# The pad at the top of SBUF of a decoder trunk grows from 96 to 224 bytes

## The chip, the cores and the metric

The kernel runs on one core of a Trainium2 chip. The metric is the device time of one execution in microseconds (us); the time of a kernel is the median of its runs. A profile comes from one further execution, whose own time is given beside it. In the profile PE is TensorE (matmuls), PEld its weight loads, DVE is VectorE, ACT is ScalarE, POOL is GpSimd, SP is SyncE, which issues most DMAs.

## What is computed

A decoder trunk of one layer on 1024 tokens of width 1024, in float32: an RMS norm, two token mixers in parallel (a gated linear recurrence and a chunked linear attention) merged by gates, an output projection and a residual; then a norm, a squared-ReLU MLP with 4096 hidden channels, a residual and a last norm. Cut to its frame:

```python
def reference(x, ..., norm_mix, ..., norm_mlp, w_up, w_down, norm_final):
    h = rms_norm(x, norm_mix)
    x = x + hybrid_mixer(h, ...)                       # w_in: 1024 x 8192, then w_out
    h = rms_norm(x, norm_mlp)
    x = x + jnp.square(jax.nn.relu(h @ w_up)) @ w_down # 1024 x 4096, 4096 x 1024
    return rms_norm(x, norm_final)
```

## The kernel before

**Three matmuls for one product.** TensorE multiplies in a shortened float32 (fp32r). Every operand is therefore split in two (`split`, L75 to L77): H is the value cast to fp32r on ACT (L76), L is what the cast lost, made on DVE (L77). `mm3` (L113) then makes each product from three matmuls into the same PSUM bank: H·H (L115), stationary times moving as they are named, then the two mixed terms (L116, L117). Nearly all matmuls have a stationary operand of 128x128 (512 bytes of a partition's row) and a moving operand of 128x512 (2048 bytes). Before each matmul TensorE loads the stationary operand of the next one, while the matmul in flight reads its moving operand, both from SBUF.

**Stages.** The mixer takes the tokens in two halves of 512 (`hT0`, `hT1`), each in four pairs of heads: projections `pj_*` with weights `w` stationary and the normed input `hT` moving, the gates of the recurrence (`pr`, `pi`, with `xcH` and `xcL` moving), then scans and small matmuls. The output projection (`po`) follows, and the second norm (`second_norm`, L686), which leaves the MLP's input in SBUF.

The MLP multiplies by quads of 2x2 blocks with seven products in place of eight. The table `PLAN` (L658) names for each of the seven steps the PSUM bank (X, Y, Z), the combination of weights (A11, s1, s2, s3, s4, A12, A22) and that of the input (B11, t1, n2, B21, T3, B22, T4). A combination of weights is made from four raw blocks by DVE sums and then split (`quad_steps`, L749).

- *Up* (`hidden`, L804): 16 quads one after the other. For each quad seven steps, each of four slices by three matmuls, 84 in all. The weights are stationary, the input h2 (14 tiles, `h2B11H` to `h2T4L`) moves. While quad q runs, DVE and ACT prepare the weights of quad q + 1, empty the banks of q (`e`, `b`) and split the hidden values of q − 1 (`hidden_ops`), which go to DRAM for all quads but the last two.
- *Down* (L936): eight blocks of two quads, 168 matmuls each. Now the hidden values `u` are stationary and the weights move. Of each two quads, one lives in the pools on the left of SBUF, the other in those on the right (`side`, L901); for each product and each block of rows, six matmuls (two row blocks by three) of the left quad are followed by six of the right one. In the last half of the last block a row block stands alone, and the sides change after three. DVE adds each bank to the accumulators (`acc`, L963). `u` and weights of the next two quads come by DMA meanwhile.

**Who lies where.** The pools on the left of SBUF grow upward from low addresses, those opened with `side="right"` grow down from the top of the 224 KiB of a partition. The mixer's tiles are all on the left. Ahead of the MLP's pools on the right a tile named `pad` is taken (L673, L674) that nothing reads or writes; it pushes down everything opened on the right after it. Tiles of 2048, 4096 and 8192 bytes follow one another there, so all of them share one residue mod 512. The addresses of the built program:

| tiles | side | byte of the first | residue mod 512 before | after |
|---|---|---|---|---|
| weights `w` of the mixer, of up and of the left down quads | left | 23296 to 47872 | 256 | 256 |
| `hT`, `y` (moving or stationary in the mixer), `xcH` at 170752, `xcL` at 174848 | left | 47872 to 174848 | 256 | 256 |
| the input of up, `h2*` | right | 114560 (before) | 384 | 256 |
| `u` of the left down quads | left | 56064 to 80640 | 256 | 256 |
| `u`, weights and raw blocks of the right down quads, `acc` | right | 98176 (before) and up | 384 | 256 |

Order on each engine: program order with hints of priority; PE runs its queue in order, and DMAs of weights and of `u` go out on SP's queue.

Of the kernel before, what the change touches and what calls it, by code (L numbers as in the profile page):

```python
# [10 lines left out]
F32 = mybir.dt.float32  # L11
# [7 lines left out]
P = 128  # L19
# [22 lines left out]
def trunk(ctx: ExitStack, tc: tile.TileContext, x, wts, mlp, pv, gains, mask_f, mask_u, out):  # L42
# [8 lines left out]
    def opened(name, **how):  # L51
        cm = tc.tile_pool(name=name, bufs=1, reuse_waits="tile", **how)
        return cm.__enter__(), lambda: cm.__exit__(None, None, None)
# [617 lines left out]


    pad, close_pad = opened("pad", side="right")  # L673
    pad.tile([P, 24], F32, tag="pad", name="pad")  # L674

    h2p = [opened(f"h2{i}", side="right") for i in range(4)]
    HOME = {"T4": 0, "B22": 0, "T3": 0, "B21": 1, "n2": 2, "t1": 2, "B11": 3}
# [371 lines left out]
```

## Time and profile before

| what | value |
|---|---|
| median of three runs | 1626.46 us (1626.07 to 1626.98) |
| the profiled execution, time around all | 1627.6 us |
| its span, first to last instruction | 1625.8 us |
| mean granted TensorE clock | 0.996 |
| mixer, output projection and second norm | to 987 us |
| up | 987 to 1309 us, 1344 matmuls |
| down | 1304 to 1618 us, 1344 matmuls |

How to read what follows: a group of instructions is given by its line, engine, operation, tiles written and read (out<-in), shape and count, then its total busy time and the mean ns of one. The ends of matmuls are modelled, so a matmul of 389 ns starts its successor earlier than that; the pace is the distance between starts. The view of stretches gives, for each piece of the span, its length, then for PE, PEld, DVE, ACT and POOL the busy time with the count of instructions that touch the piece, then the granted clock (1.00 is full), the share of DMA and GB/s. Waits are given as who waited for whom, in us in total, times, and the longest one. L numbers are lines of the kernel printed above.

### The profile page before, as it was taken

What the parts mean: (1) busy time and instruction counts of PE and PEld (TensorE: products, weight loads), DVE (VectorE), ACT (ScalarE), POOL (GpSimd) and SP (SyncE); (2) the same over time, 40 slices, a digit from 0 to 9 for tenths busy, and PEclk for the clock granted to TensorE, in tenths of its full rate; (3) what the DMA queues carried; (4) which work ended last, traced back from release to release, by engine and by line L of the source; (5) the groups of instructions that cost most, each with busy time, mean ns of one, the idle gap of its engine ahead of it and who ended that gap; (6) DMA issues with size and microseconds to landing.
All of it is one profiled execution on the core that took longest, in us unless ns stands there. A gap on an engine that the chain in (4) does not pass through costs nothing.

```text
span 1625.8 us, 23177 instructions
## 1 busy us (share of the span) xinstructions
PE 1583.0 (97%) x9240; PEld 1306.5 (80%) x9240; DVE 1212.2 (75%) x1751; ACT 764.6 (47%) x1186; POOL 65.0 (4%) x99
## 2 busy tenths in 40 slices
PE   7999999999999999999999997999999999999998
PEld 6788788788788788788787876888888877888886
DVE  5975956848764865848759688977777888788876
ACT  4643545435442544436434566766776732222113
POOL 0010100100100000000100100000000000000000
PEclk9999999999999999999999998999999999999999
DMA  6212212122243222222122362666656575666652
GB/s 237 91 66 91 92 66 104 66 91 92 79 167 135 86 78 90 80 78 103 67 91 91 117 207 104 248 248 250 237 233 246 223 269 213 256 255 247 256 209 104
DMA packets 57996, 246.51 MB, mean 152 GB/s; under 512 B 6688, under 2 KB 6816, under 8 KB 47136
## 3 DMA queue, kind: packets, MB, share of 16 engines
q1 hardware_dynamic: 56304, 239.27, 39.4%
q10 hardware_dynamic: 1584, 5.77, 1.0%
q8 instruction: 72, 1.18, 0.3%
q14 instruction: 36, 0.29, 0.1%
HBM read 185.24 MB, written 59.77 MB: 151 GB/s over the span
## 4 chain that ended last, share of the span: by engine, by line
PE 80%; DVE 15%; DMA 2%; issue 1%; ACT 1%; POOL 0%; DVEq 0%; POOLq 0%; SPq 0%; ACTq 0%
PE uX L115 3%; PE uX L117 3%; PE dX L115 3%; PE uX L116 3%; PE dX L117 3%; PE dX L116 3%; DVE wL L77 2%; PE pj_ga L117 2%; PE pv L116 2%; PE pv L117 2%; PE pv L115 2%; PE pj_ga L115 2%; PE pj_ga L116 2%; PE pj_f L117 2%; PE pj_ma L115 2%; PE pj_ma L117 2%
## 5 line engine op out<-in xcount | busy, mean ns | idle before, releaser
L77 DVE TENSOR_TENSOR wL<-raw,wH 128x1024 fp32r<-128x1024 f32 x160 | 194.3, 1214 | 150.0 <-ACT wH L76 145.8
L76 ACT CAST wH<-raw 128x1024 fp32r<-128x1024 f32 x160 | 167.8, 1049 | 166.3 <-issue 66.4
L963 DVE TENSOR_TENSOR acc<-acc,dX 128x512 f32<-128x512 f32 x128 | 85.1, 682 | 30.4 <-PE dX L117 29.7
L76 ACT CAST wA<-q 128x512 fp32r<-128x512 f32 x32 | 19.8, 621 | 129.0 <-PE dX L117 102.1
L963 DVE TENSOR_TENSOR acc<-acc,dY 128x512 f32<-128x512 f32 x64 | 43.5, 685 | 16.0 <-PE dY L117 15.1
L345 DVE RECIPROCAL rr<-rr 128x512 f32<-128x512 f32 x16 | 53.5, 3346 | 0.0
L823 ACT ACTIVATE b<-b 128x512 f32<-128x512 f32 x48 | 30.2, 631 | 38.4 <-DVE b L822 38.3
L115 PE MATMUL pv<-wH,hT0H 128*128 128x256 f32 x128 | 37.7, 294 | 0.0
L116 PE MATMUL pv<-wL,hT0H 128*128 128x256 f32 x128 | 37.4, 293 | 0.0
L117 PE MATMUL pv<-wH,hT0L 128*128 128x256 f32 x128 | 37.4, 292 | 0.0
L115 PE MATMUL pv<-wH,hT1H 128*128 128x256 f32 x128 | 36.5, 285 | 0.0
L116 PE MATMUL pv<-wL,hT1H 128*128 128x256 f32 x128 | 36.2, 283 | 0.0
L117 PE MATMUL pv<-wH,hT1L 128*128 128x256 f32 x128 | 36.2, 283 | 0.0
L311 DVE SCALAR_TENSOR_TENSOR xc<-xp,pvt,xc 128x512 f32<-128x512 f32 x48 | 33.1, 746 | 0.0
L551 ACT ACTIVATE on<-po 128x128 f32<-128x128 f32 x64 | 17.0, 278 | 33.4 <-PE po L541 33.2
L570 ACT ACTIVATE smb<-pj_mb 128x512 f32<-128x512 f32 x16 | 9.6, 597 | 45.4 <-PE pj_mb L117 45.2
L824 ACT ACTIVATE b<-b 128x512 f32<-128x512 f32 x48 | 30.0, 630 | 1.1
L77 DVE TENSOR_TENSOR wA<-q,wA 128x512 fp32r<-128x512 f32 x32 | 21.9, 686 | 10.5 <-ACT wA L76 10.3
L565 ACT ACTIVATE g<-pj_g 128x512 f32<-128x512 f32 x16 | 9.6, 599 | 37.3 <-PE pj_g L117 37.3
L444 POOL TENSOR_SCALAR seg<-seg 128x128 f32<-128x128 f32 (+1 forms) x16 | 12.7, 792 | 360.4 <-DVE seg L384 360.4
L384 DVE TENSOR_TENSOR seg<-seg 128x128 f32<-128x128 f32 (+2 forms) x96 | 26.7, 305 | 0.2
L117 PE MATMUL pj_ga<-hT1H,wL 128*128 128x512 f32 x64 | 26.5, 414 | 0.0
(1854 smaller groups left out, 5264.3 us busy)
## 6 DMA issues: line engine op xcount, KB each, us to landing
raw<-wts_in SPq DMA_DIRECT2D x160, 512.0 KB, 3.4
q<-mlp_in SPq DMA_DIRECT2D x64, 512.0 KB, 4.0
x<-x_in SPq DMA_DIRECT2D x8, 512.0 KB, 5.8
acc<-x ACTq DMA_DIRECT2D x8, 512.0 KB, 6.5
y_out<-acc SPq DMA_DIRECT2D x16, 256.0 KB, 2.1
xs<-x_in SPq DMA_DIRECT2D x8, 256.0 KB, 3.3
x<-xs SPq DMA_DIRECT2D x8, 256.0 KB, 2.4
x2s<-x_in SPq DMA_DIRECT2D x4, 512.0 KB, 4.4
```

Of the source, the lines that this page charges most:

```text
L76: keep(A.copy(h, src))
L77: keep(V.tensor_tensor(out=lo, in0=src, in1=h.bitcast(F32), op=ALU.subtract))
L115: PE.matmul(o, ah, bh, start=first, stop=False, **how)
L116: PE.matmul(o, ah, bl, start=False, stop=False, **how)
L117: PE.matmul(o, al, bh, start=False, stop=last, **how)
L311: V.scalar_tensor_tensor(xc[:, s, :], xp[:, j : j + T], pvt[:, PV_CW + 8 * j + u : PV_CW + 8 * j + u + 1], xc[:, s, :], op0=ALU.mult, op1= ...
L345: V.reciprocal(rec, rec)
L384: mul = lambda o, a, b: V.tensor_tensor(out=o, in0=a, in1=b, op=ALU.mult)
L551: A.activation(on[:, 4 * s + n, :], po[:, n * P : (n + 1) * P], AF.Square, accum_out=ssq[:, 4 * s + n : 4 * s + n + 1])
L823: A.activation(b[:, at, :], b[:, at, :], AF.Relu, scale=-1.0 if at == 2 else 1.0)
L824: A.activation(b[:, at, :], b[:, at, :], AF.Square)
L963: V.tensor_tensor(out=dst, in0=dst, in1=banks[bk, pr], op=op)
```

## The change

```diff
     pad, close_pad = opened("pad", side="right")
-    pad.tile([P, 24], F32, tag="pad", name="pad")
+    pad.tile([P, 56], F32, tag="pad", name="pad")
```

The pad has 56 float32 a partition in place of 24, which is 224 bytes in place of 96. Each of the 142 tiles on the right starts 128 bytes lower; each tile on the left stays. The two built programs have the same instructions in the same order on every engine, with the same waits; only the addresses differ.

## The prediction

> **What bounds the kernel now.** I read the page first, for who is busy and who ends the run.
>
> ```profile
> span 1625.8 us, 23177 instructions
> PE 1583.0 (97%) x9240; PEld 1306.5 (80%) x9240; DVE 1212.2 (75%) x1751; ACT 764.6 (47%) x1186; POOL 65.0 (4%) x99
> PE 80%; DVE 15%; DMA 2%; issue 1%; ACT 1%; POOL 0%; DVEq 0%; POOLq 0%; SPq 0%; ACTq 0%
> ```
>
> TensorE holds 80% of the chain that ended last. A busy PE is not a PE at its peak, so the question is at what pace matmuls of one shape (128x128 stationary, 128x512 moving) start. The change moves addresses and nothing else, so I compare stretches whose two operands lie differently. Next comes the view of stretches (length, then busy time and count of each engine, granted clock, DMA share, GB/s); the first stretch is mixer, two are the up half of the MLP, two the down half.
>
> ```profile
> 854.73:878.76 24.03, 24.03 (x107) 19.90 (x106) 21.71 (x26) 16.61 (x21) 0.00 (x0) 1.00 0.26 94
> 1201.17:1239.97 38.80, 38.80 (x169) 31.31 (x167) 30.68 (x39) 27.16 (x38) 0.00 (x0) 1.00 0.62 243
> 1240.27:1279.24 38.97, 38.97 (x168) 31.22 (x167) 30.75 (x39) 27.11 (x38) 0.00 (x0) 1.00 0.62 242
> 1354.38:1602.55 248.17, 248.17 (x1089) 204.64 (x1087) 197.85 (x289) 51.87 (x67) 0.00 (x0) 1.00 0.56 220
> 1590.00:1600.00 10.00, 10.00 (x45) 8.26 (x44) 6.22 (x13) 7.22 (x19) 0.00 (x0) 1.00 0.01 2
> ```
>
> PE never idles in them and the clock is full (1.00). The counts include one or two matmuls that straddle an edge, so the pace comes from the starts, here from the timeline of PE (start, duration, line, operation); I counted the starts between first and last row of each stretch: 106, 167, 167 and 1087.
>
> ```profile
> 854.73 0.39 PE L116 MATMUL pr<-xcL,wH 128*128 128x512 f32 x1
> 878.76 0.39 PE L116 MATMUL pj_g<-hT1L,wH 128*128 128x512 f32 x1
> ...
> 1201.17 0.39 PE L116 MATMUL uX<-h2T3L,ws310H 128*128 128x512 f32 x1
> 1239.96 0.47 PE L115 MATMUL uX<-h2T3H,ws312H 128*128 128x512 f32 x1
> 1240.27 0.40 PE L116 MATMUL uX<-h2T3L,ws312H 128*128 128x512 f32 x1
> 1279.24 0.44 PE L115 MATMUL uX<-h2T3H,ws314H 128*128 128x512 f32 x1
> ...
> 1354.38 0.40 PE L116 MATMUL dX<-ws116L,u0n 128*128 128x512 f32 x1
> 1602.55 0.43 PE L115 MATMUL dX<-ws128H,u12n 128*128 128x512 f32 x1
> ```
>
> Mixer: 24.03/106 = 226.7 ns from start to start. Up: 38.79/167 = 232.3 and 38.97/167 = 233.4 ns, mean 232.8. Down: 248.17/1087 = 228.3 ns. The addresses of the built program, in the table of placement above, sort these: in the mixer weights and moving operand both start at residue 256 mod 512, in up weights at 256 and h2 at 384, in down both at 256 for the quads kept on the left and both at 384 for those on the right, with a switch of side after every six matmuls. The switch can be seen in the groups by line of 1395 to 1436 us (mean ns of one last; L115, L116, L117 are the three matmuls of one product, u3 right side):
>
> ```profile
> L115 PE MATMUL dX<-ws119H,u3n 128*128 128x512 f32 x4 | 1.6, 391 | 0.0
> L116 PE MATMUL dX<-ws119L,u3n 128*128 128x512 f32 x4 | 1.6, 389 | 0.0
> L117 PE MATMUL dZ<-wA1219H,u3B 128*128 128x512 f32 x4 | 1.6, 392 | 0.0
> L115 PE MATMUL pi<-xcH,wH 128*128 128x512 f32 x32 | 12.4, 389 | 0.0
> L117 PE MATMUL uX<-h2B11H,wA 128*128 128x512 f32 x52 | 20.5, 395 | 0.0
> ```
>
> The durations are modelled, but they follow the pace: 389 where residues agree (mixer, and the middle matmul in down although both operands are at 384), 391 and 392 for the first and last ones, which meet a neighbour from the other side, 395 in up over 1040 to 1300 us. So it is the difference between the two residues that goes with the slower pace, not the residue 384 itself. Nor is it the high half of SBUF: the pi row reads xcH at byte 170752, weights below byte 48000, and has 389.
>
> **The change part by part.** The pad takes 128 bytes more, so everything in the pools on the right moves down by exactly 128 bytes: h2, the late u, the late weights, the late raw tiles and the accumulators go from residue 384 to 256. Order, waits and instructions of all engines stay the same. No operation is added or removed; the only price is the pace of matmuls.
>
> *Up, 1010 to 1284 us.* 1167 matmuls run there without a wait. At the mixer's pace each saves 232.8 − 226.7 = 6.1 ns: −7.1 us. Below I use −6.4 as the small end (0.6 ns each is kept) and −7.1 as the large one.
>
> *Down, 1354 to 1602 us.* No switch of residue is left: 1087 × (228.3 − 226.7) = −1.7 us; small end −1.4.
>
> *Restarts.* After a pause a matmul run takes a while to reach its pace even where residues agree. Two rows of a restart in the mixer, ten matmuls apart:
>
> ```profile
> 86.55 0.40 PE L115 MATMUL pj_mb<-hT0H,wH 128*128 128x512 f32 x1
> 88.86 0.39 PE L116 MATMUL pj_mb<-hT0L,wH 128*128 128x512 f32 x1
> ```
>
> 2.31 us for ten, 4.3 ns each over the settled pace, so some 0.04 us a restart. The two up stretches above are divided by such a pause (1239.96 to 1240.27); with five of them in up: +0.2 us, at most +0.5.
>
> *A loop that does not get faster.* That pause is PE waiting for the X bank, which ACT empties late (timeline of ACT, before the pause that begins at 1279.24):
>
> ```profile
> 1275.71 1.05 ACT L76 CAST ws115H<-s 128x1024 fp32r<-128x1024 f32 x1 [0.82 <-PE uX L116]
> 1276.67 1.04 ACT L76 CAST u13t<-b 128x1024 fp32r<-128x1024 f32 x1
> 1278.56 0.58 ACT L819 COPY e<-uX 128x512 f32<-128x512 f32 x1
> ```
>
> PE frees a buffer at 1275.71, ACT then works 3.43 us without pause to 1279.14, and PE does about 14 matmuls meanwhile. Those 14 shrink by 14 × 6.1 = 85 ns and ACT's 3.43 us do not, so each such wait may grow by 0.09 us. Seven pairs of quads: +0.6 us; between 0 (the wait is elsewhere) and +1.2 (every quad).
>
> *Stretches where PE's gain is lost.* Three waits end on other engines (waits, by total; and two stretches):
>
> ```profile
> PE uX L115 <- ACT ws30H L76: 1.7, 1, 1.7
> PEld dZ L116 <- DVE wA1230L L77: 1.6, 1, 1.6
> ACT wA L76 <- DMA q<-mlp_in: 17.8, 1, 17.8
> 1284.40:1312.90 28.50, 27.39 (x116) 21.25 (x114) 27.76 (x36) 21.47 (x31) 0.00 (x0) 1.00 0.61 221
> 1312.90:1354.10 41.20, 40.53 (x173) 32.11 (x173) 34.97 (x50) 10.38 (x13) 0.00 (x0) 1.00 0.75 287
> ```
>
> The first holds PE until 1009.6 whatever it did before (about 58 matmuls, 0.3 us). In 1284 to 1313 DVE is busy 27.76 of 28.50 us and PE waits for its last split, so 110 faster matmuls (0.6 us) only wait longer. In 1313 to 1354 the reloaded weights come 17.8 us late by DMA and PE pauses at the end (165 matmuls, 0.6 us). I take 0 for all three; if none were bound they would give 1.5 us.
>
> *Tail, 1602.8 to 1615.9 us.* Single row blocks, so the side switches every three matmuls:
>
> ```profile
> 1602.82:1615.85 13.03, 13.03 (x58) 10.48 (x56) 11.56 (x22) 4.10 (x12) 0.00 (x0) 1.00 0.36 135
> ```
>
> 13.03/56 = 232.7; aligned it saves 56 × 6.0 = 0.3 us, and DVE (11.56 of 13.03) takes some of it back: −0.15.
>
> Elsewhere the cover holds: DVE's 30.75 us and ACT's 27.11 us of a pair of quads must fit in 168 × 226.7 ns = 38.1 us instead of 39.3.
>
> Sum: −7.1 − 1.7 − 0.15 + 0.2 + 0.6 = −8.2 us. The profiled execution took 1627.6 us around its span of 1625.8, 1.1 above the median, and I carry the difference over: span 1617.6, median 1626.46 − 8.2 = **1618.2 us**. Large end: 7.1 + 1.7 + 0.3 + 1.5 = 10.6, 1615.8. Small end: 6.4 + 1.4 − 0.5 − 1.2 = 6.1, 1620.4.
>
> **The rivals.**
>
> *No change: addresses do not matter.* Up could be slower for another reason that mixer lacks: DMA at 0.62 against 0.26, or DVE and ACT writing. For it: nothing in the trace shows an address. Against it: down has DMA 0.56 over the long stretch and 0.01 in 1590 to 1600, and x45 in 10.00 us there is the same 228 pace; and in down 389 and 392 alternate with the side. Then 1626.5. The Trainium skill speaks for this rival. Its page "SBUF — State Buffer", section "Who interferes with whom", says that PE and ACT never wait on anyone, and "TensorE: Matmul & The Clock Gate", section "Step-by-step: what each phase is for", says that loading the next tile's weights does not steal SBUF read bandwidth from the running matmul; by them the residues could not matter and the sum would be 0. The 232.8 against 226.7 ns of equal shapes at full clock disagrees.
>
> *Only the switches go.* Up is slow for its own reason and keeps 232.8; down gains 1.7 and the tail 0.15: 1624.6. Against it: up and mixer have the same slices of 512 and 2048 bytes.
>
> *Slower: equal residues without settling.* The restart rows show that equal residues alone do not give 226.7; the two read streams first have to fall into step. If h2 at its new place never does, all 2254 matmuls of up and down run at one unsettled pace p. The change loses from p = 230.6 on (where 1167 × (232.8 − p) = 1087 × (p − 228.3)); at the 233.4 of the slower up stretch it costs 1167 × 0.6 + 1087 × 5.1 = +6.2 us: 1632.7. For it: the ten slow matmuls above. Against it: the mixer settles every time, in down both sides settle within a matmul or two of a switch.
>
> **How the numbers follow.** The main case gets 0.84, no change 0.06, only the switches 0.04, slower 0.06. The range is the main case's, 1615.8 to 1620.4; it leaves out the other cases (0.16) and little more. A measurement of this kernel tells about 0.2% (3.3 us) from no change; the main case lies beyond that even at its small end, the second and third within: faster 0.84, same 0.10, slower 0.06.
>
> **What would show it.** The up matmuls' mean falls from 395 to 389 ns and two quads take 38.1 to 38.4 us; in down L115, L116 and L117 all have 389. The waits at 1009.6 and for wA1230L grow by 0.3 to 0.6 us, that at the X bank by about 0.1 each. Mixer stretches and all DVE and ACT durations stay. It is wrong if up keeps 395 (another cause than residues), if the 389 comes but the span falls by under 6 us (another engine takes it), or if anything ahead of 977 us moves.

## The result and the profile after

| kernel | median, us | runs (lowest to highest) | ratio to before, 95% interval | span of the profiled run |
|---|---|---|---|---|
| before | 1626.35 | 6 (1625.81 to 1627.95) | | 1625.8 |
| after | 1619.67 | 6 (1618.12 to 1621.45) | 0.9958 [0.9946, 0.9971] | 1619.5 |

The changed kernel is faster, by 6.7 us in this first measurement. Two later ones gave 1626.91 to 1619.22 and 1627.33 to 1618.76 (both among the experiments), so 7.7 and 8.6 us; the mean of the three is 7.7. The forecast was 1618.2 us, 8.2 less than before.

The page of after, its span, its busy times and the chain that ended last:

```profile
span 1619.5 us, 23177 instructions
PE 1573.0 (97%) x9240; PEld 1302.9 (80%) x9240; DVE 1211.3 (75%) x1751; ACT 763.0 (47%) x1186; POOL 66.8 (4%) x99
PE 77%; DVE 17%; DMA 2%; ACT 2%; issue 2%; POOL 0%; DVEq 0%; POOLq 0%; SPq 0%; ACTq 0%
```

The instruction counts are those of before. PE is busy 10 us less; DVE, ACT and POOL are within 2 us of what they had. The stretches of after that answer to those of the prediction come next: mixer, two quads of up (the 167 starts from the same instruction to the same instruction), down (1087 starts), tail (56 starts).

```profile
855.28:879.33 24.05, 24.05 (x108) 19.90 (x106) 21.73 (x26) 16.62 (x21) 0.00 (x0) 1.00 0.28 93
1238.58:1276.55 37.97, 37.97 (x169) 31.16 (x167) 30.62 (x39) 26.93 (x38) 0.00 (x0) 1.00 0.64 247
1350.03:1596.48 246.45, 246.45 (x1089) 203.84 (x1087) 197.24 (x289) 51.84 (x67) 0.00 (x0) 1.00 0.56 221
1596.81:1609.61 12.80, 12.80 (x58) 10.44 (x56) 11.53 (x22) 4.10 (x12) 0.00 (x0) 1.00 0.35 136
```

The mixer is as before (24.05 against 24.03 us). Two quads of up went from 38.97 to 37.97 us, which is 233.4 to 227.4 ns a matmul; down from 248.17 to 246.45 us, 228.3 to 226.7 ns; the tail from 13.03 to 12.80 us. The groups by line say the same. First up (1040 to 1270 us) of after, then down (1390 to 1431 us) of after; the last number ahead of the second bar is the mean ns of one:

```profile
L115 PE MATMUL uX<-h2B11H,wA 128*128 128x512 f32 x48 | 18.7, 389 | 0.0
L117 PE MATMUL uX<-h2B11H,wA 128*128 128x512 f32 x48 | 18.7, 389 | 0.0
```

```profile
L115 PE MATMUL dX<-ws119H,u3n 128*128 128x512 f32 x4 | 1.6, 389 | 0.0
L117 PE MATMUL dZ<-wA1219H,u3B 128*128 128x512 f32 x4 | 1.6, 389 | 0.0
```

395 is gone from these rows of up, and 391 and 392 from those of down: they now have the mixer's 389. In up only the first matmuls behind a wait for the X bank stay longer (394 to 422 ns in the mean of four).

**Where the gain sits.** Five instructions cut the MLP into pieces. Their starts are in the timeline of PE (start, duration, line, operation; in brackets the wait ahead of it and who ended it). Before (the start of ws314H, 1279.24, stands in the prediction):

```profile
1009.62 0.51 PE L115 MATMUL uX<-h2T3H,ws30H 128*128 128x512 f32 x1 [1.72 <-ACT ws30H L76]
1312.91 0.50 PE L116 MATMUL dZ<-wA1230L,u14B 128*128 128x512 f32 x1 [1.12 <-DVE wA1230L L77]
1354.04 0.50 PE L115 MATMUL dX<-ws116H,u0n 128*128 128x512 f32 x1 [0.20 <-DVE acc L963]
1617.93 0.39 PE L117 MATMUL dX<-wA1229H,u13t 128*128 128x512 f32 x1
```

After, the profile of the first measurement:

```profile
1010.60 0.50 PE L115 MATMUL uX<-h2T3H,ws30H 128*128 128x512 f32 x1 [1.95 <-ACT ws30H L76]
1276.55 0.50 PE L115 MATMUL uX<-h2T3H,ws314H 128*128 128x512 f32 x1
1309.68 0.51 PE L116 MATMUL dZ<-wA1230L,u14B 128*128 128x512 f32 x1 [0.89 <-DVE wA1230L L77]
1349.69 0.50 PE L115 MATMUL dX<-ws116H,u0n 128*128 128x512 f32 x1 [0.28 <-DVE acc L963]
1611.73 0.40 PE L117 MATMUL dX<-wA1229H,u13t 128*128 128x512 f32 x1
```

After once more, the profile of its third measurement (e10):

```profile
1009.98 0.50 PE L115 MATMUL uX<-h2T3H,ws30H 128*128 128x512 f32 x1 [1.95 <-ACT ws30H L76]
1273.67 0.50 PE L115 MATMUL uX<-h2T3H,ws314H 128*128 128x512 f32 x1
1306.82 0.50 PE L116 MATMUL dZ<-wA1230L,u14B 128*128 128x512 f32 x1 [0.90 <-DVE wA1230L L77]
1347.03 0.50 PE L115 MATMUL dX<-ws116H,u0n 128*128 128x512 f32 x1 [0.25 <-DVE acc L963]
1609.13 0.39 PE L117 MATMUL dX<-wA1229H,u13t 128*128 128x512 f32 x1
```

Differences of these starts:

| piece | before | after | e10 | e10 − before |
|---|---|---|---|---|
| start to ws30H (mixer, norm, first product) | 1009.62 | 1010.60 | 1009.98 | +0.36 |
| ws30H to ws314H (up) | 269.62 | 265.95 | 263.69 | −5.93 |
| of it: starts up to 260 ns apart, excess over 226.7 | 6.95 | 0.31 | 0.22 | −6.73 |
| of it: starts further apart (waits), excess | 0.83 | 3.80 | 1.62 | +0.79 |
| ws314H to wA1230L | 33.67 | 33.13 | 33.15 | −0.52 |
| wA1230L to ws116H | 41.13 | 40.01 | 40.21 | −0.92 |
| ws116H to the last matmul (down) | 263.89 | 262.04 | 262.10 | −1.79 |

The third and fourth rows are sums over the 1155 distances between successive starts of that piece. The pace of up and of down is very nearly the mixer's in both profiles of after. What differs between these two profiles of one program, 2.3 us in up, lies in the starts that are further apart: in the first there is a stretch at half clock, and one raw block that came late. The view of stretches shows the first of these, two times 3 us from the start of ws30H, in after and then in e10 (the granted clock is the third number from the end):

```profile
1010.60:1013.60 3.00, 2.94 (x8) 2.12 (x9) 2.49 (x3) 0.00 (x0) 0.00 (x0) 0.69 0.04 5
1013.60:1016.60 3.00, 3.00 (x11) 2.35 (x11) 0.61 (x1) 0.00 (x0) 0.00 (x0) 0.74 0.91 341
```

```profile
1009.98:1012.98 3.00, 2.93 (x12) 2.10 (x13) 2.50 (x3) 0.00 (x0) 0.00 (x0) 1.00 0.02 1
1012.98:1015.98 3.00, 3.00 (x15) 2.48 (x14) 0.69 (x1) 1.36 (x3) 0.00 (x0) 1.00 0.93 345
```

The clock stays at 0.5 for some 3.4 us there (0.31 × 3 + 0.26 × 3 = 1.71 us of full clock are missing, which half clock takes 3.4 us to lose). Six matmuls start 0.42 to 0.43 in place of 0.23 us apart, the one ahead of them and the one behind are late too: the first 30 distances from ws30H on take 8.85 us, in e10 7.31, so the stretch takes 1.5 us.

### The profile page after: what moved, and what is told of

Read it like the earlier page. It is cut to its first block, busy times and chain, and to the rows that moved or that the text cites. A ratio compares the mean times of both kernels' runs of the same rounds, so it can differ in the third digit from the quotient of the medians.

```text
span 1619.5 us, 23177 instructions
## 1 busy us (share of the span) xinstructions
PE 1573.0 (97%) x9240; PEld 1302.9 (80%) x9240; DVE 1211.3 (75%) x1751; ACT 763.0 (47%) x1186; POOL 66.8 (4%) x99
## 4 chain that ended last, share of the span: by engine, by line
PE 77%; DVE 17%; DMA 2%; ACT 2%; issue 2%; POOL 0%; DVEq 0%; POOLq 0%; SPq 0%; ACTq 0%
PE dX L115 3%; PE dX L116 3%; PE dX L117 3%; PE uX L115 3%; PE uX L117 3%; PE uX L116 3%; DVE wL L77 2%; PE pj_ga L117 2%; PE pj_ga L116 2%; PE pj_ga L115 2%; PE pv L115 2%; PE pv L117 2%; PE pv L116 2%; PE pj_f L117 2%; PE pj_ma L117 2%; PE pj_ma L116 2%
```

## The experiments

Each kernel is compared with before in the same series. Residues are those of the built programs, mod 512 unless another is named.

**Again, unchanged (e1, e10).**

> The changed kernel once more, to see what of its profile is its own and what changes from run to run. If the wait on a weight load near 1199 us (1.1 us) and the half clock near 1012 us (3.4 us long) are chance, one or both are elsewhere or gone here and the median is 1618 to 1620 us; if the change itself brings them, both stand at the same place again and the span is within 1 us of 1619.5. Mixer stretches as before; up at 389 ns mean, 226.7 ns start to start.

> The kernel after, unchanged. Both theories: 1619.2 +- 0.7. If the half-clock stretch at 1009 to 1015 us comes with this program and not by chance, its profile shows it a third time, with the first matmul of ws31H some 1.2 to 1.5 us later against ws30H than in the run with both sides at 384.

Measured: e1 1619.22 us (1618.47 to 1620.25, 4 runs) against 1626.91, ratio 0.9950 [0.9935, 0.9965]; e10 1618.76 us (1617.81 to 1619.54, 5 runs) against 1627.33, ratio 0.9946 [0.9933, 0.9960]. The half-clock stretch is in the profile of e1, at 1009 to 1013 us, and not in that of e10. So it comes and goes with one program, and a single profile of after can be 1.5 us longer for it.

**Both sides at 384 (e2).** The old pad, and a tile that nothing uses at the bottom of SBUF, so that everything on the left rises by 128 bytes.

```diff
+    lpad = const.tile([P, 32], F32, tag="lpad", name="lpad")
...
-    pad.tile([P, 56], F32, tag="pad", name="pad")
+    pad.tile([P, 24], F32, tag="pad", name="pad")
```

> The pad stays at 96 bytes and everything on the left moves up by 128 bytes, so that both sides lie at residue 384. Theory (the difference of the residues of stationary and moving operand sets the pace): up at 226.7 ns start to start, 389 ns mean, in down L115, L116 and L117 all at 389, mixer unchanged, 1618 to 1621 us. Rival (384 is a bad residue, 256 a good one): up stays at 395 and the mixer rises from 389 to 395 too, over 1630 us.

Measured: 1618.01 us (1617.47 to 1619.20, 4 runs), ratio 0.9943 [0.9928, 0.9958]. Its two quads of up and its 1087 starts of down:

```profile
1235.16:1273.12 37.96, 37.96 (x168) 31.16 (x166) 30.62 (x39) 26.89 (x38) 0.00 (x0) 1.00 0.65 249
1346.71:1593.12 246.41, 246.41 (x1089) 203.84 (x1087) 197.17 (x289) 51.86 (x67) 0.00 (x0) 1.00 0.57 222
```

Both are those of after (37.97 and 246.45). All MLP operands on the right lie exactly where they lay before, at the residue 384; what moved is what they are multiplied with. So the place of an operand does not count, the distance between the two operands does.

**One half alone (e3, e4).** A second pad, opened just ahead of the late `u` (and so after h2), moves the tiles of the right down quads alone: in e3 back to residue 384 while h2 stays at 256, in e4 (with the old first pad) to 256 while h2 stays at 384.

```diff
+    pad2, close_pad2 = opened("pad2", side="right")
+    pad2.tile([P, 96], F32, tag="pad2", name="pad2")
...
-close_late_u, close_pad, close_ust
+close_late_u, close_pad2, close_pad, close_ust
```

That is e3; e4 has `[P, 32]` there and `[P, 24]` in the first pad.

> h2 at residue 256 as in the changed kernel, but a second pad of 384 bytes ahead of the late pools puts the right side of down back to 384. Theory: up at 389, down keeps 391, 389 and 392 (228.3 ns start to start), 1.5 to 2 us more than the changed kernel: 1620 to 1622.5 us. Rival (the gain of down comes from elsewhere, by its DMA or DVE): the same as the changed kernel, 1618 to 1620.

> h2 stays at residue 384, a second pad of 128 bytes ahead of the late pools puts the right side of down to 256. Theory: up keeps 395 (232.8 ns start to start), down L115, L116, L117 all 389 (226.7 ns), 1.5 to 2.5 us less than before: 1624 to 1625 us. Rival: down unchanged, 1626 to 1627.

Measured: up alone 1621.06 us (1620.29 to 1623.11, 5 runs), ratio 0.9964 [0.9950, 0.9978]; down alone 1624.82 us (1623.73 to 1625.95, 10 runs), ratio 0.9986 [0.9977, 0.9995], both against 1626.91. Up and down of e3, then of e4:

```profile
1235.46:1273.40 37.94, 37.94 (x169) 31.17 (x167) 30.63 (x39) 26.96 (x38) 0.00 (x0) 1.00 0.65 248
1347.20:1595.33 248.13, 248.13 (x1088) 204.67 (x1087) 197.78 (x289) 51.85 (x67) 0.00 (x0) 1.00 0.56 221
```

```profile
1240.45:1279.26 38.81, 38.81 (x169) 31.32 (x167) 30.75 (x39) 27.16 (x38) 0.00 (x0) 1.00 0.64 243
1352.91:1599.98 247.07, 246.69 (x1088) 203.81 (x1086) 197.18 (x289) 51.85 (x67) 0.00 (x0) 1.00 0.56 221
```

The gain of up goes with h2 (37.94 against 38.81), that of down with the late tiles (248.13 against 247.07, of which 0.6 us are waits that after lacks). The two gains add: 5.85 + 2.09 = 7.9 us, against 7.7 for both together in that series.

**Other distances (e5, e6, e7, e11, e12).** Only the width of the pad changes: `[P, 88]`, `[P, 120]`, `[P, 40]`, `[P, 8]` and `[P, 48]` in place of `[P, 56]`; the left side stays at 256.

> Pad of 352 bytes: the right side lies at residue 128, 128 bytes under the left instead of 128 over it. Theory (the difference counts, whatever its sign): up near 395 ns mean, 232 to 234 ns start to start, down 391/389/392 as before, 1625 to 1628 us. Rival (only a moving operand ahead of the stationary one is slow): up at 389, about 1620 us.

> Pad of 480 bytes: right side at residue 0, half of 512 away. If the cost grows with the distance of the residues, up is slower than 395 ns mean (over 234 ns start to start) and the time over 1628 us; if any difference costs the same, up is 394 to 396 and the time 1625 to 1628; if only the residue mod 256 counts, up is at 389 and the time about 1619.

> Pad of 160 bytes: right side at residue 320, 64 bytes over the left. If the cost grows with the distance, up lies between 389 and 395 ns mean (229 to 231 ns start to start) and the time near 1622 us; if any difference costs the same, 395 and 1625 to 1628; if 64 bytes are too few to matter, 389 and about 1619.

> Pad of 32 bytes: the right side at residue 448, 192 from the left side's 256. If only the distance mod 256 counts and its sign does not, 192 is as good as 64 the other way: up 229 ns from start to start, down about 231, near 1626.8 us. If the two streams collide where one runs ahead of the other, the sign counts: up and down differ from the 229 and 231 measured at +64.

> Pad of 192 bytes: the right side at residue 288, 32 from the left side's 256. If the cost grows with the distance from a multiple of 256, up has 227 to 229 ns and down 227 to 230: 1619 to 1625 us. If any distance that is no multiple of 256 costs the same as 128, up has 232.8 and the time is near 1627.

Measured, one run each; the paces are from the starts, the mean of those up to 260 ns apart:

| kernel | residue on the right | right minus left, mod 256 | up, ns | down, ns | time, us | before in that series |
|---|---|---|---|---|---|---|
| after | 256 | 0 | 227.0 | 226.7 | 1619.67 | 1626.35 |
| e6 | 0 | 0 | 226.9 | 226.7 | 1619.16 | 1626.94 |
| e12 | 288 | 32 | 233.3 | 230.0 | 1629.17 | 1627.33 |
| e7 | 320 | 64 | 229.0 | 230.3 | 1626.75 | 1626.94 |
| before | 384 | 128 | 232.8 | 228.3 | 1626.35 | |
| e5 | 128 | 128 | 233.3 | 228.2 | 1627.00 | 1626.94 |
| e11 | 448 | 192 | 233.3 | 230.3 | 1633.92 | 1627.33 |

Down of e6, of e7 and of e11, 1087 starts each:

```profile
1347.86:1594.31 246.45, 246.45 (x1089) 203.84 (x1087) 197.28 (x289) 51.86 (x67) 0.00 (x0) 1.00 0.56 222
```

```profile
1351.44:1601.84 250.40, 250.40 (x1089) 203.96 (x1088) 198.15 (x289) 51.84 (x67) 0.00 (x0) 1.00 0.55 218
```

```profile
1358.50:1608.88 250.38, 250.38 (x1089) 203.94 (x1087) 197.91 (x289) 51.82 (x67) 0.00 (x0) 1.00 0.55 218
```

Three things follow, each from single profiles. A distance of 256 is as good as 0, and 128 and −128, the same mod 256, cost the same within 0.5 ns: what counts is the distance mod 256, not mod 512. The cost does not grow with the distance: 32 costs up as much as 128 does. And the sign counts: in up, 64 costs 2.3 ns a matmul and 192, which is −64 mod 256, costs 6.6. e7's time, 1626.75 us, lies where the second case written down for it put the time, but by luck: up is at 229.0 ns, as in the first case, and down, for which no case had a price, loses 2.0 ns a matmul against before; its profile also holds the half-clock stretch.

Down shows the sign in another way. There every switch from left to right has one sign and every switch back the other, so 64 and −64 must cost the same in sum, and they do (250.40 and 250.38 us). Laid out by the place of a matmul among the six of its side (mean ns from its start to the next one, between 1395 and 1590 us, 60 groups of each side that have a switch ahead of them and behind):

| kernel, side | 1st | 2nd | 3rd | 4th | 5th | 6th, to the other side |
|---|---|---|---|---|---|---|
| before, left | 230.5 | 227.0 | 227.0 | 226.0 | 227.0 | 232.5 |
| before, right | 230.5 | 227.0 | 227.0 | 226.0 | 227.0 | 232.4 |
| e7 (64), left | 230.7 | 235.5 | 228.5 | 232.0 | 230.5 | 225.8 |
| e7 (64), right | 228.3 | 229.1 | 233.3 | 235.9 | 224.1 | 231.7 |
| e11 (−64), left | 228.3 | 229.2 | 233.3 | 235.8 | 224.2 | 231.7 |
| e11 (−64), right | 230.8 | 235.9 | 228.3 | 232.5 | 230.9 | 225.8 |

With the sign turned, left and right swap their rows, to 0.1 ns in one pair of rows and to 0.5 in the other. At 128 only the switch itself and the matmul after it lose, 5.8 and 3.8 ns; at 64 the whole six are disturbed. e11's time has two things in it beside this: its first up matmul starts 2.5 us later than before's (989.59 against 987.05 us), and a half-clock stretch like that of after takes some 1.6 us. The 2.5 us arise in the output projection, whose matmuls read tiles on the left alone: at 945.1 us a wait for the second norm is 0.9 us longer than in before (2.00 against 1.11), and a half-clock stretch follows (945.5 to 948.9 us). Its 1633.92 is therefore no measure of the distance; its paces are. e12 differs from the others in one thing more: 288 is no multiple of 64.

**The copy that frees the X bank goes first (e8, e9).** In after, ACT makes three casts between PE's release of a buffer and the copy `e` (L819) that empties the X bank. The third of them, in before, is the row that belongs between the last two of the prediction's ACT rows:

```profile
1277.61 1.05 ACT L76 CAST u13n<-b 128x1024 fp32r<-128x1024 f32 x1
```

A hint of priority moves that copy ahead of two of them; no work is added or left out.

```diff
-            A.copy(e_of[q, step], o)
+            with tc.high_priority(200):
+                A.copy(e_of[q, step], o)
```

> The changed kernel, with ACT's copy out of the X and Y banks in up (L819) at a priority of 200, so that it stands ahead of two 1.05 us casts on ACT. Theory (what the changed kernel leaves is PE's wait for the X bank behind ACT's casts, 2.9 to 3.4 us in all): those eight waits go, 1.5 to 3 us less than the changed kernel, 1616 to 1618 us. Rival (the wait only moves to the casts that now come later, the hidden values or weights): within 0.7 us of the changed kernel.

> The kernel after with the copy that frees the X bank moved ahead on ACT, run a second time, beside the kernel after in the same call. Theory: the X-bank waits cost up some 1.3 to 1.8 us and moving the copy gives most of them back, so this is 1 to 2 us faster than the kernel after of this call (some 1617.5 against 1619). Rival: the first look was lucky (no half-clock stretch near 1012 us in it); then the medians of the two lie within 0.5 us and the intervals overlap.

ACT in e8, ahead of the same X-bank product as in the prediction's rows (the copy has become L820):

```profile
1268.30 1.04 ACT L76 CAST ws115H<-s 128x1024 fp32r<-128x1024 f32 x1
1269.24 0.58 ACT L820 COPY e<-uX 128x512 f32<-128x512 f32 x1
1269.72 1.06 ACT L76 CAST u13t<-b 128x1024 fp32r<-128x1024 f32 x1
```

And two of the starts that cut the MLP, in e8:

```profile
1009.26 0.50 PE L115 MATMUL uX<-h2T3H,ws30H 128*128 128x512 f32 x1 [1.96 <-ACT ws30H L76]
1304.68 0.50 PE L116 MATMUL dZ<-wA1230L,u14B 128*128 128x512 f32 x1 [1.06 <-DVE wA1230L L77]
```

Between them lie 295.42 us, against 296.84 in e10: 1.4 us less, in which the waits of PE up to ws314H (distances over 260 ns) fell from 1.62 to 0.53 us. In e9 it is 296.89, with a half-clock stretch that takes 1.5 us of it. The hint also moves three matmuls of the Y bank to the other side of the first X ones in some quads, so the start of ws314H itself isn't the same point in these two kernels. The times: e8 1618.42 us (1616.70 to 1619.80, 4 runs) against 1626.94, ratio 0.9949 [0.9932, 0.9965]; e9 1618.40 us (1618.25 to 1621.82, 5 runs) against 1627.33, ratio 0.9949 [0.9937, 0.9962]. Beside the 1618.76 of after in e9's own series this is 0.36 us and the runs overlap: the wait is shown and can be taken away, but that the kernel as a whole gets faster by it is not shown.

## Why the prediction was right, step by step

*Up, −7.1 (small end −6.4), and restarts, +0.2.* Right: the excess over the mixer's pace was 6.95 us by count, and 0.22 and 0.31 us of it are left, which is the restarts' share: in e8, where PE hardly waits for the X bank, 0.02 us is left. e3 shows that h2's place alone brings the gain. Two quads, from the first start of ws312H to that of ws314H, take 38.3 us, where 38.1 to 38.4 was forecast (39.3 before).

*The loop that does not get faster, +0.6.* Right in kind, a little small: waits in up went from 0.83 to 1.62 us in e10, +0.8 (+0.9 in e2). The waits of 985 to 1310 us, before and then e10, name the X bank (total, times, longest):

```profile
PEld uX L115 <- ACT e L819: 1.6, 7, 0.2
```

```profile
PEld uX L115 <- ACT e L819: 2.8, 8, 0.5
```

Each grew by 0.12 us on average (1.6/7 to 2.8/8) where 0.09 was forecast, and e8, where the copy no longer stands behind the casts, has one of 0.2 us left. Not all of the +0.8 is such a wait. In e10 the first start behind the bank comes 0.28 to 0.29 us after the one ahead of it (0.23 to 0.24 in before) and the second one 0.34 us after that (0.27 to 0.31 in before), so half of the usual growth of 0.1 us lies in the second start, which the prediction had under restarts; and 0.2 us more come from one bank (ws310H, 0.49 us).

*Down, −1.7, and tail, −0.15.* Right: 248.17 to 246.45 is −1.72; 13.03 to 12.80 is −0.23. e4 alone brings it.

*Three stretches at 0.* The first is right: the wait at ws30H grew from 1.72 to 1.95 us (0.3 to 0.6 more was forecast) and swallowed what PE gained ahead of it. At the other two the forecast was that the faster matmuls only wait longer; but the wait for wA1230L fell from 1.12 to 0.90 us, and the stretches are 0.5 and 0.9 us shorter in e10. That part did not come true, though it is not shown that the faster pace is what shortens them. In e5, where up and down are as slow as before, the two starts are these:

```profile
1313.53 0.50 PE L116 MATMUL dZ<-wA1230L,u14B 128*128 128x512 f32 x1 [1.09 <-DVE wA1230L L77]
1353.51 0.50 PE L115 MATMUL dX<-ws116H,u0n 128*128 128x512 f32 x1
```

That is 39.98 us between them, 1.15 less than before, at the old pace. In the three profiles of after this piece takes 40.01, 40.70 and 40.21 us, so it differs by 0.7 us within one program, and from 39.73 to 41.18 over all kernels: a term of 0.9 us can't be read from single profiles of it. The piece from ws314H to wA1230L is another matter. It takes 33.13, 33.13 and 33.15 us in the three profiles of after and 33.71 in both of the kernel with the copy first, so it repeats within a program; between kernels it does not follow the pace of up, with 33.16 us in e4 and 33.21 in e12, where up is slow, and 33.52 in e3, where it is fast. Its 0.5 us may belong to the change, by another way than the pace of up; with one profile of before this stays open.

*The sum.* Up −5.9 and down with its tail −1.8, the two pieces that follow the distance, make −7.7 us, which is the mean of the three measurements (7.7). That the two agree so closely is in part luck, since the measurements themselves lie 1.9 us apart and the two pieces above are left out. The forecast of −8.2 is 0.5 larger: up's pace with its restarts was put 0.2 too high (−6.9 for −6.7) and its waits 0.2 too low. The 1619.67 of the first measurement is 1.5 above the forecast. Its profile (1621.3 us around a span of 1619.5) has 1.5 us of half clock, which no step of the prediction had; 0.6 us from one raw block (its load landed 7.1 us after its issue, against a median of 4.0, and two starts of PE lie 1.09 us apart at 1199 us, 0.49 at the same place in e10); and 0.98 us by which everything ahead of ws30H was later than before, where e10 has 0.36. The first two are absent in the profile of e10, whose runs have the median 1618.76. The third is scatter ahead of the change: the mixer's rows at 853 us already start 0.4 us later in e10 than before and 0.0 us later in e2, at the same pace. The prediction had named anything that moves ahead of 977 us as a sign against it. A matmul of the output projection that starts at 977.12 us before comes 0.95 us later in after, 0.37 later in e10 and 1.22 earlier in e1, three profiles of one program: the sign came up, but it does not come from the addresses.

*What the prediction read from the addresses* was right as far as it went: it is the difference of the two residues that costs, not 384 itself (e2) and not the half of SBUF. It took the difference mod 512, and there the rule was too narrow: 256 apart is as good as equal (e6). The pairs of before that it compared have only 0 and 128, so they could not show it.

*The rivals.* No change falls with e2, e3 and e4: nothing but addresses differs, and the pace follows them. The two rules of the Trainium skill that were weighed there, that PE waits on no one ("SBUF — State Buffer", section "Who interferes with whom") and that loading the next weights takes no read bandwidth from the running matmul ("TensorE: Matmul & The Clock Gate", section "Step-by-step: what each phase is for"), do not fit 226.7 against 232.8 to 233.3 ns for equal shapes at full clock. Only the switches go falls with after's 227.0 ns in up; its price was right, as e4 gives that case by itself. Slower falls too: at its new place h2 runs at the mixer's pace. That two read streams fall into step after a pause, as that rival had it, no run shows; the runs show only that starts behind a pause are slow, the second one above all (0.34 us after the first).

Why a distance costs what it does isn't shown. That left and right swap their rows when the sign turns says that the cost is set by the addresses and the order, without chance. Two streams of reads, the weights being loaded and the operand in flight, that hinder each other at some distances would fit this, but no run here sees the reads themselves.

## What to carry to other kernels

Where matmuls of one shape run at two paces in one profile at full clock and with no wait between them, sort them by the byte addresses of their stationary and moving operands: here equal residues mod 256 were worth 6 ns of 233 a matmul, and a pad of 128 bytes on either side was all it took. Trying half the distance is no half measure: 32 bytes apart was as bad as 128 in up, and 32 and 64 were worse than 128 in down. When such a gain is summed, take it over the pieces that PE itself bounds and take off what waits for buffers that another engine empties will grow by (0.8 of 6.7 us here).

## What the runs showed of the hardware that was not expected

- With fp32r operands of 128x128 and 128x512, the distance from start to start is 226.7 ns where the two addresses agree mod 256 (mixer, and down of after), and in up 229.0 (64 apart), 232.8 to 233.3 (128 apart) or 233.3 (32 apart, and −64) where they don't. It is signed: 64 and −64 differ by 4.3 ns.
- A stretch of half clock of 3.4 us followed the wait at ws30H (1.7 to 2.0 us, 2.1 to 2.4 us from start to start) in 5 of 14 profiles (after, e1, e7, e9, e11), at three different placements, and didn't in e8 (the program of e9) and e10 (the program of after). It costs 1.4 to 1.6 us each time. The Trainium skill, page "TensorE: Matmul & The Clock Gate", section "HAM oscillation — how this bites in real kernels", puts the rule as no idle gaps over about 3.4 us; here the stretch came behind shorter ones.
- Whether it comes goes with the moment at which the pause falls. The half-clock stretches stand on a raster of 3.41 us: in each of the five profiles this one starts nine times 3.41 us after the one at the start of up begins, and both last a whole number of 3.41 us. After shows it so (the granted clock is the third number from the end):

```profile
981.04:987.86 6.82, 3.36 (x15) 3.02 (x16) 5.94 (x9) 3.86 (x10) 1.72 (x2) 0.50 0.40 154
1011.76:1015.17 3.41, 3.35 (x9) 2.64 (x9) 1.33 (x3) 0.00 (x0) 0.00 (x0) 0.50 0.45 153
```

  With that raster laid through all 14 profiles, the pause ahead of ws30H (from 0.23 us after the last start) begins between 0.1 us before and 0.5 us after a point of it in the five, and 1.1 to 2.4 us after one in the nine others. Why a pause of 1.8 us in e12 that begins 1.1 us after a point, and ends ahead of the next, brings none is not shown.
- Single profiles do not settle a term under 1 us in the piece from wA1230L to ws116H, which reloaded weights end: one program gave 40.01, 40.70 and 40.21 us.
